# Reordering the opening of a one-core transformer block: four token tiles' first half, then the products of two weight groups

## The chip, the core and the metric

The kernel runs on one core of a Trainium2 chip. The core has five engines with a queue each: TensorE (PE in the profile; PEld is its weight load), VectorE (DVE), ScalarE (ACT), GpSimd (POOL) and SyncE (SP, which here only issues transfers). An engine takes its queue in order, and an instruction that waits for another engine holds up everything behind it. SBUF is the working memory; PSUM holds what TensorE writes (this kernel keeps eight tiles of 128 x 512 float32 there, one to a bank). The metric is the device time of one execution in microseconds (us).

## The reference

One encoder layer on x of 1024 tokens x 1024 features:

```
h = layer_norm(x, ln_in_g, ln_in_b)
proj = h @ w_in                      # 1024 x 11776
att  = dilated_attention(q, k, v of proj)
rec  = hgrn2(q, f_fwd, f_bwd, i, g of proj)
merged = sigmoid(ga) * (att @ w_att_up) + sigmoid(gh) * (rec @ w_hgrn_up)
h = layer_norm(ALPHA * h + merged @ w_o, ln1_g, ln1_b)
h = layer_norm(ALPHA * h + swiglu(h), ln2_g, ln2_b)
```

The change is in the first two lines and in where the normalised x is taken from for `ALPHA * h`.

## The kernel before

**Precision.** Every float32 operand of a matmul is split into a high part (`hi`, a cast on ScalarE, L205) and a low part (`lo`, a subtraction on GpSimd or VectorE, L209). A product of two split operands is three matmuls (`mm3`, L255 to L257): hi·hi, hi·lo, lo·hi.

**Blocks.** The product with `w_in` is done by a Strassen-Winograd scheme of seven products instead of eight, on 2 x 2 blocks. The activations are transposed (features on partitions). `b11` and `b21` are the two halves of the features for tokens 0 to 511 (token tiles 0 to 3, 128 tokens each), `b12` and `b22` those for tokens 512 to 1023 (tiles 4 to 7), and `t1` = b12 - b11, `t2` = b22 - t1, `t3` = b22 - b12, `t4` = b21 - t2 are their sums. The weights of a pair of column tiles are `a11`, `a12`, `a21`, `a22` (512 x 128 each, one DMA of 256 KB each in `block`), with the sums `s1` to `s4`. `PRODUCTS` pairs them: product 1 is a11·b11, 2 is a12·b21, 6 is s2·t2, 5 is s1·t1, 7 is s3·t3, 3 is s4·b22, 4 is a22·t4. Each product is 4 x 3 = 12 matmuls of 128 x 128 by 128 x 512.

**The stream of products.** `stream` is a generator. A weight group n is two pairs of column tiles (g = 0, 1); there are 23 groups. The order within a group is `ORDER` = 1, 2, 6, 5, 7, 3, 4, each product for g = 0 and then for g = 1. `prep(i)` writes the split of product i's weights three products ahead (four buffers each for `w_hi` and `w_lo`), `sums` the weight sums, `bank` picks the PSUM bank, `keep` copies a bank to SBUF, and the functions of `tiles` carry the results out (`evac`).

**The opening.** `phase0` loads the eight tiles of x, takes the statistics of each (`bn_stats` on VectorE, the power -0.5 on GpSimd), normalises it on ScalarE, stores the normalised tile to `ah_d` in DRAM, transposes it on TensorE by halves of 512 features (`transposed`, L285), scales the four 128 x 128 pieces of a half out of PSUM (`v`, partly on ScalarE, L293, partly on VectorE, L295: `on_act` says which), and splits the blocks. Tiles 4 to 7 also form t1 to t4. In the text of the program the eight tiles come one after the other, both halves each, with two products put in after four tiles.

**What sets the order.** The program is written once, and a list scheduler that models the engines puts each engine's instructions in order. Parts of the code written under `high_priority` go ahead; `add_manual_dep` (in `ordered` and `behind`) fixes that one instruction stands behind another. So the text does not tell the order, and below it is shown as the built program has it.

**Later.** `phase1` runs the stream and, between products, the recurrence and the attention as "side" work. Near its end `residual` reads the normalised x back, scales it and stores it to `ahs_d` for the second layer norm.

## Time and profile before

| | us |
|---|---|
| median of 3 runs | 2134.19 |
| the three runs | 2123.66 to 2137.27 |
| the profiled execution, time | 2131.49 |
| the profiled execution, span | 2129.7 |
| PE busy in the span | 2029.0 (95%) |
| DVE, POOL, ACT busy | 1392.7, 1077.5, 919.7 |

The span runs from the first to the last instruction of the profiled execution; its own time is 1.8 us longer. A busy PE is one that has a matmul under way, which says nothing of the clock it runs at: the granted clock stands apart. The views are read in stretches of the span, since the opening, where PE starts and stops, is a small part of it.

### The profile page before, as it was taken

The page shows a single profiled execution, that of the slowest core. Times are in us where ns is not written, and L with a number is a line of the kernel's source. Part 1 is how long each engine was busy: PE and PEld are TensorE (multiplying, and loading weights), DVE is VectorE, ACT ScalarE, POOL GpSimd, SP SyncE. Part 2 cuts the span into 40 slices and gives each one's busy share as a digit, 9 for nine tenths or more (in the row PEclk, how much of TensorE's full clock was granted, in tenths as well). Part 3 has the DMA queues.
Part 4 walks back from the last instruction along what each step waited for, and adds up shares of the span by engine and source line. Part 5 has one row for each costly group of instructions (what it writes and reads, how often), then busy time and mean ns, then how long its engine had stood idle before and what let it go on. Part 6 is the DMA issues. An engine that isn't in the chain of part 4 may idle for free.

```text
span 2129.7 us, 30900 instructions
## 1 busy us (share of the span) xinstructions
PE 2029.0 (95%) x10941; PEld 1674.6 (79%) x10941; DVE 1392.7 (65%) x2228; ACT 919.7 (43%) x1864; POOL 1077.5 (51%) x882
## 2 busy tenths in 40 slices
PE   4799999999999999999999899999999999999998
PEld 3678787788878788887888688878788888887876
DVE  7667746777459753788536712337867677767778
ACT  6544455434544435543355432135433333343542
POOL 3466653567536664465644754443656566630012
PEclk9899999999999999999999999999999999999999
DMA  5342442435424343333444755244434344348423
GB/s 202 109 133 95 147 155 73 144 118 167 130 92 141 135 146 125 124 129 109 146 130 142 283 188 164 89 139 139 154 109 153 129 144 134 117 160 291 158 89 124
DMA packets 273885, 301.10 MB, mean 141 GB/s; under 512 B 14081, under 2 KB 205378, under 8 KB 273730
## 3 DMA queue, kind: packets, MB, share of 16 engines
q1 hardware_dynamic: 266272, 273.73, 39.7%
q10 hardware_dynamic: 7458, 25.40, 3.0%
q8 instruction: 86, 1.41, 0.3%
q14 instruction: 69, 0.57, 0.1%
HBM read 200.25 MB, written 98.83 MB: 140 GB/s over the span
## 4 chain that ended last, share of the span: by engine, by line
PE 77%; DVE 12%; issue 5%; POOL 3%; DMA 2%; ACT 2%; SPq 0%; ACTq 0%; DVEq 0%; POOLq 0%
PE pj L255 17%; PE pj L256 17%; PE pj L257 16%; PE sd L256 6%; PE sd L255 6%; PE sd L257 6%; PE sd L1049 2%; POOL w_lo L209 1%; DVE qd L964 1%; DVE qd L967 1%; PE sd L998 1%; DVE p L849 1%; PE sd L863 1%; DVE fb L953 1%; ACT p L827 1%
## 5 line engine op out<-in xcount | busy, mean ns | idle before, releaser
L209 POOL TENSOR_TENSOR w_lo<-wa,w_hi 128x512 fp32r<-128x512 f32 x276 | 377.4, 1374 | 297.9 <-ACT w_hi L205 274.0
L205 ACT CAST w_hi<-wa 128x512 fp32r<-128x512 f32 x276 | 170.4, 619 | 245.8 <-PE pj L256 159.5
L209 POOL TENSOR_TENSOR w_lo<-wsum,w_hi 128x512 fp32r<-128x512 f32 x88 | 129.0, 1474 | 113.0 <-PE sd L257 60.4
L200 POOL TENSOR_TENSOR mv<-mv,mhalf 128x1 f32<-128x1 f32 x24 | 15.5, 647 | 228.6 <-DVE mv L199 225.5
L209 POOL TENSOR_TENSOR w_lo<-f_raw,w_hi 128x512 fp32r<-128x512 f32 x66 | 102.1, 1555 | 55.4 <-ACT w_hi L205 54.2
L255 PE MATMUL pj<-xt1hi,w_hi 128*128 128x512 f32 x260 | 103.9, 400 | 16.3 <-ACT xt1hi L205 10.7
L205 ACT CAST w_hi<-wsum 128x512 fp32r<-128x512 f32 x88 | 54.7, 621 | 124.6 <-PE sd L256 114.4
L255 PE MATMUL pj<-xb22hi,w_hi 128*128 128x512 f32 x260 | 102.6, 394 | 1.1 <-ACT wkeep L511 1.1
L256 PE MATMUL pj<-xt1lo,w_hi 128*128 128x512 f32 x260 | 102.3, 393 | 0.0
L257 PE MATMUL pj<-xt1hi,w_lo 128*128 128x512 f32 x260 | 102.0, 392 | 0.0
L256 PE MATMUL pj<-xb22lo,w_hi 128*128 128x512 f32 x260 | 101.5, 390 | 0.0
L257 PE MATMUL pj<-xb22hi,w_lo 128*128 128x512 f32 x260 | 101.3, 390 | 0.0
L209 POOL TENSOR_TENSOR w_lo<-ws,w_hi 128x512 fp32r<-128x512 f32 x46 | 63.0, 1373 | 69.2 <-ACT w_hi L205 63.3
L205 ACT CAST gwsum<-a_raw 128x512 fp32r<-128x512 f32 (+1 forms) x78 | 47.8, 616 | 102.9 <-PE pj L256 48.0
L511 ACT COPY wkeep<-pj 128x512 f32<-128x512 f32 x138 | 80.1, 582 | 22.1 <-DVE evh L430 10.1
L403 DVE TENSOR_TENSOR evh<-wkeep,pj 128x512 f32<-128x512 f32 x66 | 57.5, 879 | 48.5 <-PE pj L257 35.2
L209 DVE TENSOR_TENSOR gwkeep<-a_raw,gwsum 128x512 fp32r<-128x512 f32 (+1 forms) x78 | 57.7, 739 | 43.1 <-ACT gwsum L205 40.2
L489 POOL TENSOR_TENSOR wa<-wa,wa 128x512 f32<-128x512 f32 x46 | 67.6, 1480 | 35.6 <-DVE ws L488 27.6
L414 DVE TENSOR_TENSOR evh<-wkeep,pj 128x512 f32<-128x512 f32 x48 | 32.6, 681 | 80.7 <-PE pj L257 65.5
L255 PE MATMUL pj<-xt4hi,w_hi 128*128 128x512 f32 x192 | 77.8, 406 | 5.6 <-DVE evh L403 5.6
L257 PE MATMUL pj<-xt2hi,w_lo 128*128 128x512 f32 x192 | 76.1, 397 | 4.9 <-POOL w_lo L209 4.9
L255 PE MATMUL pj<-xb11hi,w_hi 128*128 128x512 f32 x192 | 77.3, 404 | 2.6 <-DVE evh L414 1.4
(406 smaller groups left out, 6587.1 us busy)
## 6 DMA issues: line engine op xcount, KB each, us to landing
wa<-in_w_in_dram SPq DMA_DIRECT2D x184, 256.0 KB, 3.1
f_raw<-in_w_ffn_in_dram SPq DMA_DIRECT2D x44, 512.0 KB, 4.2
a_raw<-gd SPq DMA_DIRECT2D x30, 512.0 KB, 3.5
gd<-fc SPq DMA_DIRECT2D x44, 256.0 KB, 2.0
gd<-fs SPq DMA_DIRECT2D x33, 256.0 KB, 2.1
tg<-evh SPq DMA_DIRECT2D x32, 256.0 KB, 3.5
tg<-tg SPq DMA_DIRECT2D x16, 512.0 KB, 3.7
y<-ahs SPq DMA_DIRECT2D x16, 512.0 KB, 5.5
```

What stands on the lines that cost most here:

```text
L205: nc.scalar.copy(hi, src)
L209: ins = e.tensor_sub(lo, src, hi.bitcast(F32))
L255: nc.tensor.matmul(ps, whi, xhi, start=first, stop=False, **kw)
L256: nc.tensor.matmul(ps, whi, xlo, start=False, stop=False, **kw)
L257: nc.tensor.matmul(ps, wlo, xhi, start=False, stop=last, **kw)
L403: self.left(nc.vector.tensor_tensor(o, self.order_src(add, g, kind), s, OP.add))
L414: self.left(nc.vector.tensor_add(t, add, ps))
L489: nc.gpsimd.tensor_sub(a["a21"], a["a11"], a["a21"])
L511: nc.scalar.copy(t, ps)
L827: nc.scalar.activation(z, z, AF.Exp, bias=N0[p, hd, tt:tt + 1], scale=QSCALE, accum_out=L0[p, hd, tt:tt + 1])
L849: nc.vector.tensor_scalar(z, z, W0[p, hd, tt:tt + 1], None, op0=OP.mult)
L1049: nc.tensor.matmul(po[:, jj, :], l, r, start=(n == 0), stop=(n == len(terms) - 1))
```

## The change

Six things, all in or for the opening:

1. `phase0` is written anew. It does the first half (b11) of tiles 0 to 3 first, then the products of b11, then their second half (b21), then tiles 4 to 7. The products are drawn from the stream inside it.
2. `stream` begins with product 1 of weight groups 0 and 1 and product 2 of groups 0 and 1, eight products in all, and then takes the other five of each group. Group 1's `a11` and `a12` are loaded for this into tiles of their own (`wfirst`) and loaded once more for its sums later. Some products go to the other PSUM banks (`sd`).
3. `transposed` gives a bank of four pieces to one engine (all four on ScalarE, or all four on VectorE), or takes two banks where both engines share a half (tile 3).
4. The three small steps behind the statistics go to GpSimd; the scale and shift are kept for all tiles (`mv0`).
5. The normalised tiles are no longer stored to `ah_d`. `residual` reads x again and normalises it once more on ScalarE.
6. `behind` and `ordered` fix some places: transposes of the second half behind the last product drawn, statistics of tiles 4 to 7 behind certain splits, the casts of the first weights behind certain casts of b11. The small parameters are loaded and transposed in two parts.

```diff
-    def transposed(self, pool, n, q, g, b, v=None, bufs=2, on_act=(1, 3, 6)):
+    def transposed(self, pool, n, q, g, b, v=None, bufs=2, on_act=(1, 3, 6), two=False, gate=None):
         ps = self.ps_sd()
+        pa = self.ps_sd() if two else ps
         for k in range(4):
-            nc.tensor.transpose(ps[:, 128 * k:128 * (k + 1)], n[:, 128 * (4 * q + k):128 * (4 * q + k + 1)],
-                                self.ident)
+            p = pa if 4 * q + k in on_act else ps
+            ins = nc.tensor.transpose(p[:, 128 * k:128 * (k + 1)], n[:, 128 * (4 * q + k):128 * (4 * q + k + 1)],
+                                      self.ident)
+            if gate:
+                self.behind(ins, gate)
...
+        def stats(tt):
+            st = self.tiny.tile([128, 2, 6], F32, name="bn0", tag="bnst", bufs=3)
+            for j in range(2):
+                ins = nc.vector.bn_stats(st[:, j, :], xs[tt][0][:, HALF * j:HALF * (j + 1)])
+                if tt > 3:
+                    self.behind(ins, at["lo", 3, "b11" if tt < 6 else "b21"])
+            mv = self.mv0[:, tt, :]
+            nc.vector.bn_aggr(mv[:, 0:2], st)
+            nc.gpsimd.tensor_scalar(mv[:, 2:3], mv[:, 1:2], LN_EPS, None, op0=OP.add)
+            nc.gpsimd.tensor_tensor(mv[:, 2:3], mv[:, 2:3], self.mhalf[:, 0:1], OP.pow)
+            nc.gpsimd.tensor_scalar(mv[:, 3:4], mv[:, 0:1], mv[:, 2:3], -1.0, op0=OP.mult, op1=OP.mult)
...
+        turn(3, 0, v[3][0], (2, 3))
+        put(3, "b11", v[3][0])
+        self.gates = [at["hi", 1, "b11"]] * 2 + [at["hi", 3, "b11"]] * 2
+        run(2)
+        for tt in range(4):
+            if tt < 3:
+                norm(tt + 1, 1)
+            turn(tt, 1, v[tt][1], DVE if tt % 2 else ACT, self.product)
+            self.left(put(tt, "b21", v[tt][1]))
             if tt == 1:
-                self.rest()
-            mv = self.stats(pool, xt, "0")
-            self.normalise(pool, xt, xt, mv)
-            nc.scalar.dma_start(self.ah_d[tt], xt)
...
+                load(2)
+                run()
+                stats(4)
+        self.rest()
+        run(3)
+        for tt in range(4, 8):
+            b11, b21 = v[tt - 4]
+            norm(tt, 0)
+            norm(tt, 1)
+            t1, t2 = xs[tt][1]
             _, (b12, b22) = hold("vt")
-            self.transposed(pool, xt, 0, gc, bc, b12, on_act=(0, 1, 3))
+            turn(tt, 0, b12, DVE if tt % 2 else ACT)
             nc.vector.tensor_sub(t1, b12, b11)
-            put("t1", t1)
-            self.transposed(pool, xt, 1, gc, bc, b22, on_act=(4, 5, 7))
+            if tt < 7:
+                stats(tt + 1)
+            turn(tt, 1, b22, ACT if tt % 2 else DVE)
             nc.vector.tensor_sub(t2, b22, t1)
-            put("t2", t2)
...
+            put(tt, "t2", t2)
+            nc.gpsimd.tensor_sub(b12, b22, b12)
+            nc.vector.tensor_sub(b21, b21, t2)
+            v[tt] = t1, b12, b22, b21
+            if tt > 4:
+                late(tt - 1, 0)
+            run()
+        late(7, 0)
+        for i in range(1, 4):
+            for tt in range(4, 8):
+                late(tt, i)
...
     def residual(self, pool, vecs):
...
-            nc.sync.dma_start(a, self.ah_d[tt])
+            nc.sync.dma_start(a, self.x[128 * tt:128 * (tt + 1), :])
+            mv = self.mv0[:, tt, :]
+            nc.scalar.activation(a, a, AF.Identity, bias=mv[:, 3:4], scale=mv[:, 2:3])
             nc.vector.scalar_tensor_tensor(a, a, ALPHA, gb, op0=OP.mult, op1=OP.mult)
...
-        seq = [(n, g, p) for n in range(len(tiles) // 4) for p in self.ORDER for g in range(2)]
+        O = self.ORDER
+        order = [(n, (p,)) for p in O[:2] for n in (0, 1)]
+        order += [(n, O[2:] if n < 2 else O) for n in range(len(tiles) // 4)]
+        seq = [(n, g, p) for n, part in order for p in part for g in range(2)]
...
+            if n == 1 and p == 2:
+                first[g, 2] = self.block(1, g, "a12", pool)
             with early(n):
                 ready[i] = self.granules()
-                self.split(*ready[i], A[g][self.PRODUCTS[p][0]])
+                self.split(*ready[i], first[g, p] if n == 1 and p < 3 else A[g][self.PRODUCTS[p][0]],
+                           key="w" if i < 4 else None)
...
-        def bank(n, g, b):
-            return self.ps_pj(2 * g + (n + b) % 2)
+        def bank(n, g, p):
+            if (n, p) in ((0, 5), (0, 2), (1, 2)):
+                return self.ps_sd()
+            return self.ps_pj(2 * g + (n + (p == 1)) % 2)
```

In `turn` the argument `act` lists the pieces that ScalarE takes (`ACT` is all four, `DVE` none), and `late` splits t1, t3, b22 and t4 of a tile. Line numbers of the changed program are some 11 to 120 higher: L255 to L257 are L268 to L270 there, L285 is L300, L205 is L212, L209 is L220, L295 is L312.

**The start of TensorE's queue**, before: transposes of x (`xt`) into PSUM (`sd`), and then the first product.

```order
L174 MATMUL sd<-tabs_sb,vrows 128x65
L285 MATMUL sd<-tabs_sb,xt 128x128 x40
L255 MATMUL pj<-xb11hi,w_hi 128x512 x2
L285 MATMUL sd<-tabs_sb,xt 128x128 x8
L256 MATMUL pj<-xb11lo,w_hi 128x512
L257 MATMUL pj<-xb11hi,w_lo 128x512
```

The same place in the changed program.

```order
L181 MATMUL sd<-tabs_sb,vrows_254 128x16
L300 MATMUL sd<-tabs_sb,xt 128x128 x16
L268 MATMUL pj<-xb11hi,w_hi 128x512 x3
L269 MATMUL pj<-xb11lo,w_hi 128x512
L270 MATMUL pj<-xb11hi,w_lo 128x512
```

Forty-eight of the 64 transposes stood ahead of the first whole product; now 16 do, and the other 48 stand between products.

**TensorE's queue where the first products of tokens 512 to 1023 come**, before: the end of product 2 of group 0 (the fourth product of the program), and what follows it.

```order
L256 MATMUL pj<-xb21lo,w_hi 128x512
L257 MATMUL pj<-xb21hi,w_lo 128x512
L255 MATMUL pj<-xt1hi,w_hi 128x512 x2
L255 MATMUL pj<-xt2hi,w_hi 128x512 x2
L256 MATMUL pj<-xt1lo,w_hi 128x512
```

In the changed program: the end of product 2 of group 1 (the eighth product), the last eight transposes, and product 6 of group 0.

```order
L269 MATMUL sd<-xb21lo,w_hi 128x512
L270 MATMUL sd<-xb21hi,w_lo 128x512
L300 MATMUL sd<-tabs_sb,xt 128x128 x8
L268 MATMUL pj<-xt2hi,w_hi 128x512 x2
L269 MATMUL pj<-xt2lo,w_hi 128x512
```

Four products of group 1, 48 matmuls, moved ahead of this point, and t2 is now the first block wanted of the second half of the tokens.

**VectorE's queue at that place in the changed program**: the work on tile 7 (`v_287` is its partner b11, `v_288` its b21; `vt` are the scaled pieces) up to the low part of its t2, and what stands behind.

```order
L312 TENSOR_SCALAR vt<-sd,vc 128x128 x4
L422 TENSOR_TENSOR xt<-vt,v_287 128x512
L426 TENSOR_TENSOR xt<-vt,xt 128x512
L429 TENSOR_TENSOR v_288<-v_288,xt 128x512
L220 TENSOR_TENSOR xt2lo<-xt,xt2hi 128x4x128
L220 TENSOR_TENSOR xt1lo<-xt,xt1hi 128x4x128 x2
L220 TENSOR_TENSOR xt3lo<-vt,xt3hi 128x4x128 x4
L220 TENSOR_TENSOR xb22lo<-vt,xb22hi 128x4x128 x4
L220 TENSOR_TENSOR xt4lo<-v_282,xt4hi 128x4x128
```

The low parts of t3, b22 and t4, which stood among those of t1 and t2 before, now stand behind the last t2.

**ScalarE's queue in `residual`**, before: casts of weights (`w_hi`), copies and evacuations (`wkeep`, `evh`), with the stores of `a`.

```order
L205 CAST w_hi<-wa_10853 128x512
L511 COPY wkeep<-pj 128x512
L205 CAST w_hi<-ws_11295 128x512
L374 DMA ahs_115<-a_11464 128x1024
L415 ACTIVATE evh<-evh 128x512
```

And in the changed program.

```order
L212 CAST w_hi<-wa_10851 128x512
L633 COPY wkeep<-pj 128x512
L452 ACTIVATE a_11462<-a_11462,mv_203 128x1024
L212 CAST w_hi<-ws_11293 128x512
L496 ACTIVATE evh<-evh 128x512
L452 ACTIVATE a_11535<-a_11535,mv_203 128x1024
```

A normalisation that waits for the load of its `a` now stands ahead of a cast of weights; there are eight such places. Apart from the opening and this stretch, the engines' orders are nearly the same in both programs.

251 lines of the change are left out of this document (148 added, 103 removed).

## The prediction

> **What bounds the kernel now.** I read the page's slices first, then the first 140 us in stretches of 10 and 20, then TensorE's waits there, then its single matmuls.
>
> ```profile
> PE   4799999999999999999999899999999999999998
> ```
>
> PE is busy nine tenths or more in nearly every fortieth (53 us) of the span; the first two hold the largest gap, and the change works there. The stretches, with each engine's busy time and number of instructions:
>
> ```profile
> core 0: us, PE busy (x) PEld busy (x) DVE busy (x) ACT busy (x) POOL busy (x), PEclk, DMA share, GB/s
> 30.00:40.00 10.00, 4.57 (x14) 2.65 (x14) 10.00 (x19) 7.03 (x17) 3.32 (x2) 1.00 0.09 38
> 40.00:50.00 10.00, 9.79 (x39) 8.15 (x40) 9.64 (x20) 8.31 (x18) 4.03 (x2) 1.00 0.05 17
> 50.00:60.00 10.00, 5.52 (x29) 4.32 (x27) 10.00 (x16) 9.70 (x23) 4.35 (x3) 0.95 0.16 63
> 60.00:70.00 10.00, 1.99 (x4) 1.00 (x4) 10.00 (x18) 5.42 (x10) 0.19 (x3) 0.50 0.26 79
> 70.00:80.00 10.00, 10.00 (x40) 7.89 (x39) 3.35 (x6) 3.81 (x7) 2.97 (x4) 0.87 0.11 31
> 100.00:120.00 20.00, 18.12 (x84) 14.73 (x83) 19.71 (x16) 8.88 (x16) 17.45 (x17) 1.00 0.26 93
> 120.00:140.00 20.00, 18.85 (x91) 15.68 (x90) 12.07 (x14) 10.28 (x19) 11.35 (x9) 1.00 0.61 187
> ```
>
> From 30 to 70 us VectorE never rests (39.6 of 40) and TensorE mostly does. At 70 VectorE has done its share and PE is full. So VectorE bounds the opening. TensorE's own waits up to 140 us say the same (total, times, longest): the longest product wait is for the last token tiles' t1, and after the opening it loses little.
>
> ```profile
> PE pj L255 <- ACT xt1hi L205: 10.7, 1, 10.7
> ...
> PE pj L257 <- POOL w_lo L209: 1.9, 1, 1.9
> ```
>
> The matmuls themselves (start, duration):
>
> ```profile
> 40.98 0.78 PE L256 MATMUL pj<-xb11lo,w_hi 128*128 128x512 f32 x1
> ...
> 45.39 0.40 PE L257 MATMUL pj<-xb11hi,w_lo 128*128 128x512 f32 x1
> ...
> 48.12 1.03 PE L285 MATMUL sd<-tabs_sb,xt 128*128 128x128 f32 x8
> ...
> 55.13 0.39 PE L257 MATMUL pj<-xb21hi,w_lo 128*128 128x512 f32 x1
> ```
>
> ```profile
> 66.23 1.22 PE L255 MATMUL pj<-xt1hi,w_hi 128*128 128x512 f32 x2 [10.71 <-ACT xt1hi L205]
> 69.24 1.22 PE L255 MATMUL pj<-xt2hi,w_hi 128*128 128x512 f32 x2 [1.79 <-ACT xt2hi L205]
> 70.39 0.80 PE L256 MATMUL pj<-xt1lo,w_hi 128*128 128x512 f32 x1
> 70.98 0.63 PE L257 MATMUL pj<-xt1hi,w_lo 128*128 128x512 f32 x1
> 71.41 0.63 PE L255 MATMUL pj<-xt1hi,w_hi 128*128 128x512 f32 x1
> ...
> 72.69 0.40 PE L255 MATMUL pj<-xt1hi,w_hi 128*128 128x512 f32 x1
> ...
> 76.78 0.39 PE L257 MATMUL pj<-xt2hi,w_lo 128*128 128x512 f32 x1
> ```
>
> The rows from 72.69 to 76.78 are 18 steps: 0.227 us a matmul. Before 72.69, and before 45.39, a step is 0.43 (70.98 to 71.41): half the rate. The first four products (48 matmuls: products 1 and 2 of group 0, for both pairs) end at 55.1; then PE rests 10.7 us, and runs without a gap from 72.7, when 48 + 2 + 2 + 5 = 57 matmuls are done. I measure an opening by its **lag**, the time at which PE runs unbroken less the time that its finished matmuls need at full rate: 72.7 - 57 x 0.227 = **59.7 us**. The total of matmuls doesn't change, so the change is worth the difference in lag plus what it alters later.
>
> **The change, part by part.** *First products.* The 16 transposes and the products of b11 wait for the fourth b11 cast on ScalarE.
>
> ```profile
> 9.35 1.24 ACT L278 ACTIVATE xt<-xt,mv 128x1024 f32<-128x1024 f32 x1 [2.49 <-DVE mv L277]
> ...
> 50.64 1.51 ACT L293 ACTIVATE vt<-sd,vc 128x128 f32<-128x128 f32 x4
> ```
>
> ```profile
> L205 ACT CAST w_hi<-wa 128x512 fp32r<-128x512 f32 x276 | 170.4, 619 | 245.8 <-PE pj L256 159.5
> ```
>
> Up to that cast ScalarE has seven half normalisations (0.62, half of 1.24), six pieces (0.38) and six casts (0.62): 10.3 us, from about 9.35, gives 19.7 us; before, the first low-part matmul ran at 41.0. The eight stores of the normalised tiles leave ScalarE's queue. TensorE then needs 48 x 0.227 = 10.9, 2 more at half rate, and 16 transposes between (8 take 1.03): 35 us. The first product of b21 waits for the last low part of b21, behind four `bn_stats` on VectorE, some 3 us more; 48 matmuls and 24 transposes take 14. The eighth product ends near 35 + 3 + 14 = 52 us.
>
> *t2, which decides.* What VectorE must do from 19.7 us until the low part of the last t2, by its changed queue: 34 subtractions and additions, 24 pieces, 8 `bn_stats`, 4 aggregations.
>
> ```profile
> 12.15 0.21 DVE L198 BATCH_NORM_AGGREGATE mv<-bn 128x2 f32<-128x12 f32 x1
> ...
> 36.24 1.27 DVE L191 BATCH_NORM_STATS2 bn<-xt 128x6 f32<-128x512 f32 x2
> ...
> 50.39 1.43 POOL L209 TENSOR_TENSOR w_lo<-wa,w_hi 128x512 fp32r<-128x512 f32 x1 [0.88 <-ACT w_hi L205]
> ...
> 50.58 1.78 DVE L355 TENSOR_TENSOR vt<-vt 128x512 f32<-128x512 f32 x1
> ...
> 57.29 1.63 POOL L209 TENSOR_TENSOR w_lo<-ws,w_hi 128x512 fp32r<-128x512 f32 x1 [2.17 <-ACT w_hi L205]
> ...
> 57.72 0.67 DVE L428 TENSOR_TENSOR wkeep<-wkeep,pj 128x512 f32<-128x512 f32 x1
> ...
> 58.31 1.15 DVE L209 TENSOR_TENSOR xt3lo<-vt,xt3hi 128x512 fp32r<-128x512 f32 x1
> ...
> 59.39 0.72 DVE L295 TENSOR_SCALAR vt<-sd,vc 128x128 f32<-128x128 f32 x2
> ```
>
> ```profile
> 66.05 0.68 DVE L209 TENSOR_TENSOR xb22lo<-vt,xb22hi 128x512 fp32r<-128x512 f32 x1
> ...
> 66.65 0.68 DVE L361 TENSOR_TENSOR v<-v,vt 128x512 f32<-128x512 f32 x1
> ```
>
> 34 x 0.60 (66.05 to 66.65) + 24 x 0.36 + 8 x 0.64 + 4 x 0.2 = 20.4 + 8.6 + 5.1 + 0.8 = 34.9, so 54.6 us if it never waits. It waits, though: the b21 pieces of tiles 1 and 3 need transposes that stand behind the first and second product (about 2.5 us each), the first b21 low part waits for ScalarE (1.3), ScalarE's casts for weight buffers of a running product (1 to 2): 7 us. And GpSimd gets in its way. In the rows above a VectorE subtraction that begins within a GpSimd one ends 0.54 us after it (50.58 + 1.78 = 52.36, GpSimd ended at 51.82; 59.46 and 58.92), while an operation that reads PSUM isn't held (57.72, 0.67). The stretch has 16 such GpSimd operations. Each costs between nothing and 1.1 us (1.78 - 0.68), so 0 to 18; half of them meeting a subtraction at 0.5 (1.15 - 0.68) is 4, and I take that, since a third or so of VectorE's time here is pieces, evacuations and waits. Sum: 54.6 + 7 + 4 = **65.6 us** for the first whole product of t2, with 96 matmuls done. The bounds are 55 (no wait, no collision) and 80 (all of both).
>
> *Clock.* Between 52 and 65 PE rests again, so it starts at half rate as at 40.98 (4.4 us of it until 45.39) and at 70.39 (2.3 us). With 3.4 us, 8 matmuls, the lag is 65.6 + 3.4 - 104 x 0.227 = **45.4 us**; gain 59.7 - 45.4 = **14.3 us**. The Trainium skill ("TensorE: Matmul & The Clock Gate", Part 1) says that an idle window of about 3.4 us halves the clock and that about 3.4 us of steady work restores it; that speaks against a queue with more rests in it. By that rule each slow start loses 1.7 us, where the rows lose 2.2 (4.4 us at half rate) and 1.2 (2.3); and the rest of 3 us ahead of the b21 products would only just escape a slow start of its own, with which the gain would be 12.6 us and not 14.3. The trace agrees that a long rest halves the clock (0.50 in 60 to 70 us), and no row here shows one of 3 us.
>
> *After t2.* VectorE still has 14 low parts (8.4 us); PE has 11 us of products 6 and 5 meanwhile, so these are hidden. They cost up to 8 if it had not. Product 6 of group 1 now follows group 0 at once, where products 1 and 2 gave its weight sums time, and half of it stands on GpSimd behind a step of the recurrence. Before, the same hand-over lost 20 - 18.12 + 20 - 18.85 = 3.0 us of PE in 100 to 140 us. I take the same, bounds 0 and 8.
>
> *residual.* Eight normalisations of 1.24 us come to ScalarE, each waiting in its queue for a load of x.
>
> ```profile
> 1200.00:1210.00 10.00, 7.54 (x32) 5.86 (x33) 8.81 (x8) 4.88 (x9) 8.66 (x6) 1.00 0.92 330
> 1210.00:1220.00 10.00, 7.13 (x33) 5.58 (x31) 9.93 (x8) 5.23 (x9) 7.39 (x5) 0.98 0.44 160
> ```
>
> ```profile
> DMA to landing us min/median/max: 3.8/5.7/9.1
> ```
>
> The second row is the load of `a` before (L371). ScalarE is half idle there, but casts of weights and evacuations stand behind the wait, and PE already loses 2.5 and 2.9 us in these two stretches. Bounds: nothing, if the loads have landed; 8 x (9.1 - 5.7) = 27 if each came as late as the latest. Nearest to nothing, since only three or four loads are issued shortly before: I take 2. The eight stores that go, the banks given to one engine (they remove some of the 39.6 us of VectorE's work order, not of its work) and the three small GpSimd steps lie beside VectorE's chain and count as nothing; without that cover the small steps would add to each tile's start.
>
> **Sum.** 2131.5 (the profiled execution) - 14.3 + 0 + 2 = **2119 us**. That execution is 2.7 us below the median of the runs shown, 2134.2, whose spread is 13.6; so 0.6% faster by the one, 0.7% by the other. About 1% is what a measurement of this kernel can tell from no change.
>
> **Rivals.** *VectorE's chain is shorter*: its waits overlap the collisions and t2 starts at 58. The lag is 58 + 3.4 - 23.6 = 37.8, the gain 22, the time 2110. For it: 7 and 4 us are put one after the other; against it: VectorE rests nowhere from 30 to 70 us now. Chance 0.2.
>
> *The change doesn't do what it says*: VectorE has about the same work before t2 is whole and every GpSimd operation collides; t2 starts at 80, the lag is 80 + 3.4 - 23.6 = 59.8, and the eight early products only fill time that was lost anyway: 2131.5 + 2, about 2133. For it: GpSimd has 16 operations there against seven before in 30 to 60 (2, 2 and 3 in the stretches). Chance 0.12.
>
> *Slower*: in `residual`, ScalarE waits in line for x, the casts of weights behind it come late, and TensorE stops for each. With the 27 us above, 2131.5 - 14.3 + 27 = 2144; with half the opening's gain gone as well, 2151, over 1% slower above 2153 to 2155. It decides from 14 us of added waits on. For it: TensorE's two thin stretches above, with the transfers at 330 GB/s and 0.92 of their time; against it, ScalarE's 4.88 of 10. Chance 0.08.
>
> **How the numbers follow.** The forecast has 0.60, with a range of its own of 2112 to 2127. The whole range, 2107 to 2136, takes in the short chain and the lost gain and leaves out most of the slow case. Faster by over 1% is the short chain and a little of the forecast's lower end, 0.22. Slower by over 1% is the upper part of the slow case and what I don't see, 0.07. Within 1%: 0.71.
>
> **What would show it.** PE's first matmul of b11 near 20 us and eight products done by 51 to 53; a second rest of PE until about 65, ended by xt2hi or xt2lo; unbroken matmuls from about 69; VectorE busy without a rest from 38 to 73. In `residual`, stretches of PE no thinner than 7 of 10. I am wrong if PE stops within the eight products for PSUM (`sd` is shared by transposes and products), if t2 starts before 58 or after 75, or if PE's busy time from 1160 to 1240 falls by more than 5 us.

## The result, and the profile after

The changed kernel takes **2118.1 us** (median of 6 executions, 2109.2 to 2120.4). The kernel before, timed beside it, takes 2131.9 us (6 executions, 2123.7 to 2137.3). The ratio is 0.9938, with an interval of 0.9919 to 0.9957, so the change makes the kernel about 0.6% faster. A second timing gave 2118.8 us (6 executions, 2114.7 to 2121.6) and a ratio of 0.9952 (0.9936 to 0.9967). The profiled execution took 2119.32 us with a span of 2117.4 us, which is 12.3 us less than before (2129.7). The prediction was 2119 us.

The total is as predicted. Its parts aren't. The slices of the changed kernel's page (TensorE's busy tenths in 40 slices) show where the time came from: the first slice is fuller (6 tenths, 4 before), the second has 7 as before, and elsewhere little moves.

```profile
PE   6799999999999999999999999999999999999998
```

The stretches of the changed kernel, with the columns that the stretches of before have (start and end; busy time and number of instructions of PE, PEld, DVE, ACT and POOL; PE's granted clock; DMA share; GB/s):

```profile
30.00:40.00 10.00, 7.89 (x43) 6.25 (x42) 7.00 (x12) 9.58 (x23) 4.51 (x4) 1.00 0.31 99
40.00:50.00 10.00, 8.64 (x41) 6.90 (x40) 10.00 (x21) 3.70 (x7) 8.74 (x10) 1.00 0.00 1
50.00:60.00 10.00, 5.71 (x29) 4.10 (x27) 9.96 (x12) 6.78 (x13) 6.63 (x5) 0.84 0.21 79
60.00:70.00 10.00, 0.00 (x0) 0.00 (x0) 9.42 (x17) 4.78 (x12) 3.12 (x2) 0.50 0.25 79
70.00:80.00 10.00, 9.56 (x34) 7.37 (x35) 10.00 (x16) 9.27 (x18) 2.59 (x2) 0.81 0.00 0
100.00:120.00 20.00, 19.13 (x88) 15.50 (x87) 20.00 (x14) 9.98 (x18) 19.51 (x16) 1.00 0.57 171
120.00:140.00 20.00, 20.00 (x90) 16.58 (x89) 16.07 (x16) 7.75 (x15) 15.01 (x12) 1.00 0.53 173
```

From 40 to 80 us VectorE is still the busy engine (39.4 of 40 us), and TensorE still has its long rest, now all of 60 to 70. GpSimd has become much busier in 40 to 60 (15.4 us; 8.4 before). In 100 to 140 TensorE loses 0.87 us, where it lost 3.03 before.

TensorE's waits up to 140 us (total, times, longest) and then its matmuls at the places that the prediction names:

```profile
PE pj L268 <- ACT xt2hi L212: 10.6, 1, 10.6
...
PE sd L269 <- DVE xb21lo L220: 1.4, 1, 1.4
PE sd L268 <- ACT xb21hi L212: 1.2, 1, 1.2
...
PE pj L270 <- POOL w_lo L220: 0.9, 1, 0.9
PE pj L269 <- DVE xt2lo L220: 0.4, 1, 0.4
```

```profile
19.84 1.65 PE L268 MATMUL pj<-xb11hi,w_hi 128*128 128x512 f32 x3 [2.30 <-ACT xb11hi L212]
...
37.12 0.50 PE L268 MATMUL sd<-xb21hi,w_hi 128*128 128x512 f32 x1 [1.19 <-ACT xb21hi L212]
...
41.66 0.50 PE L269 MATMUL sd<-xb21lo,w_hi 128*128 128x512 f32 x1 [1.36 <-DVE xb21lo L220]
...
53.58 0.39 PE L270 MATMUL sd<-xb21hi,w_lo 128*128 128x512 f32 x1
...
70.03 1.22 PE L268 MATMUL pj<-xt2hi,w_hi 128*128 128x512 f32 x2 [10.65 <-ACT xt2hi L212]
71.66 0.79 PE L269 MATMUL pj<-xt2lo,w_hi 128*128 128x512 f32 x1 [0.41 <-DVE xt2lo L220]
...
73.90 0.40 PE L268 MATMUL pj<-xt2hi,w_hi 128*128 128x512 f32 x1
```

The first b11 product starts at 19.84. The eighth product ends at 53.97. Then TensorE rests until t2 comes: its high part at 70.0, its low part at 71.7. From 73.90 it runs at the full rate, with 96 + 7 = 103 matmuls done. Its lag is 73.9 - 103 x 0.227 = **50.5 us**, where before it was 59.7. The opening therefore gives **9.2 us**, and not 14.3.

The other terms can be read from the **lead**: how much earlier the changed kernel's profile has the same number of products' matmuls (128x512) done. It is 11.2 us at 160 to 230 us (9.2 from the opening, about 2 from the hand-over in 100 to 140), 8.7 at 300, 8.2 at 1140, 11.1 at 1200, 9.75 at 1560 to 1860 and 12.0 at the end.

### The profile page after: what moved, and what is told of

Its sections match the earlier page's. It is cut to its first block, busy times and chain, and to the rows that moved or that the text cites. A ratio compares the mean times of both kernels' runs of the same rounds, so it can differ in the third digit from the quotient of the medians.

```text
span 2117.4 us, 30907 instructions
## 1 busy us (share of the span) xinstructions
PE 2027.0 (96%) x10942; PEld 1673.0 (79%) x10942; DVE 1396.8 (66%) x2214; ACT 925.9 (44%) x1870; POOL 1100.3 (52%) x903
## 3 DMA queue, kind: packets, MB, share of 16 engines
q8 instruction: 86, 1.41, 0.3%
## 4 chain that ended last, share of the span: by engine, by line
PE 56%; DVE 6%; DMA 2%; issue 2%; ACT 1%; POOL 1%; SPq 0%; ACTq 0%; DVEq 0%; POOLq 0%
PE pj L269 11%; PE pj L268 11%; PE pj L270 11%; PE sd L269 6%; PE sd L268 6%; PE sd L270 6%; PE sd L1158 1%; DMA a<-in_x_dram 1%; ACT p L936 1%; DVE qd L1073 1%; DVE qd L1076 0%; PE sd L1107 0%; POOL w_lo L220 0%; DVE p L958 0%; DVE fb L1062 0%
## 5 line engine op out<-in xcount | busy, mean ns | idle before, releaser
L220 POOL TENSOR_TENSOR w_lo<-wa,w_hi 128x512 fp32r<-128x512 f32 x272 | 375.3, 1387 | 286.1 <-ACT w_hi L212 256.3
L212 ACT CAST w_hi<-wa 128x512 fp32r<-128x512 f32 x272 | 167.9, 619 | 249.2 <-PE pj L269 130.8
L220 POOL TENSOR_TENSOR w_lo<-wsum,w_hi 128x512 fp32r<-128x512 f32 x88 | 128.7, 1471 | 113.5 <-PE sd L270 60.7
L220 POOL TENSOR_TENSOR w_lo<-f_raw,w_hi 128x512 fp32r<-128x512 f32 x66 | 102.0, 1554 | 55.7 <-ACT w_hi L212 54.5
L208 POOL TENSOR_TENSOR mv<-mv,mhalf 128x1 f32<-128x1 f32 x16 | 10.7, 677 | 207.3 <-DVE mv L207 207.2
L212 ACT CAST w_hi<-wsum 128x512 fp32r<-128x512 f32 x88 | 54.7, 622 | 124.8 <-PE sd L269 114.6
L268 PE MATMUL pj<-xt1hi,w_hi 128*128 128x512 f32 x252 | 101.3, 402 | 4.5 <-DVE evh L484 3.7
L268 PE MATMUL pj<-xb22hi,w_hi 128*128 128x512 f32 x252 | 99.5, 395 | 0.0
L270 PE MATMUL pj<-xt1hi,w_lo 128*128 128x512 f32 x252 | 99.3, 395 | 0.0
L270 PE MATMUL pj<-xb22hi,w_lo 128*128 128x512 f32 x252 | 98.4, 391 | 0.3 <-POOL w_lo L220 0.3
L220 POOL TENSOR_TENSOR w_lo<-ws,w_hi 128x512 fp32r<-128x512 f32 x46 | 64.7, 1411 | 64.8 <-ACT w_hi L212 60.1
L212 ACT CAST gwsum<-a_raw 128x512 fp32r<-128x512 f32 (+1 forms) x78 | 47.7, 616 | 100.6 <-PE pj L269 43.5
L268 PE MATMUL pj<-xt2hi,w_hi 128*128 128x512 f32 x192 | 78.0, 407 | 13.1 <-ACT xt2hi L212 10.6
L220 DVE TENSOR_TENSOR gwkeep<-a_raw,gwsum 128x512 fp32r<-128x512 f32 (+1 forms) x78 | 57.8, 741 | 41.0 <-ACT gwsum L212 38.1
L268 PE MATMUL pj<-xt4hi,w_hi 128*128 128x512 f32 x192 | 77.8, 405 | 5.8 <-DVE evh L484 5.8
L268 PE MATMUL pj<-xb11hi,w_hi 128*128 128x512 f32 x192 | 77.3, 404 | 3.4 <-ACT xb11hi L212 2.3
L495 DVE TENSOR_TENSOR evh<-wkeep,pj 128x512 f32<-128x512 f32 x45 | 30.7, 683 | 71.7 <-PE pj L270 49.0
```

What stands on the lines that cost most here:

```text
L212: ins = nc.scalar.copy(hi, src) if eng_hi == "act" else nc.vector.tensor_copy(hi, src)
L220: ins = e.tensor_sub(lo, src, hi.bitcast(F32))
L268: nc.tensor.matmul(ps, whi, xhi, start=first, stop=False, **kw)
L270: self.product = nc.tensor.matmul(ps, wlo, xhi, start=False, stop=last, **kw).ins.name
L495: self.left(nc.vector.tensor_add(t, add, ps))
```

## The experiments

Where a median is given, the number of executions stands behind it, and ratios are to the kernel before on the same chip. The other experiments are one profiled execution each and are read by their rows only. "t2 after b11" is the time from the first b11 product to the low part that makes t2 whole; it is used since the first b11 product alone moves by 1 us or so from run to run. In the changed kernel it is 71.6 - 19.8 = 51.8 us; in its repeat, 51.5.

**1. Only the order of the products undone.** The opening keeps its new order of tiles, engines and queues. The products go back to "group 0 whole, then group 1", and group 1's early loads of weights go with them.

```diff
-        order = [(n, (p,)) for p in O[:2] for n in (0, 1)]
-        order += [(n, O[2:] if n < 2 else O) for n in range(len(tiles) // 4)]
+        order = [(n, O) for n in range(len(tiles) // 4)]
...
-        run(3)
+        run(2)
```

> The changed kernel with one part undone: the products of each weight group stand in the order of before (group 0 whole, then group 1), so four products and not eight run ahead of t2. Theory (VectorE's chain to the last low part of t2 sets the end of the opening, and the early products fill time that TensorE would lose): the chain loses the evacuations of two products, some 3 us, so t2 is whole at 68 to 69 us and not at 71.7, but only 48 matmuls are done by then, so the lag is 57 to 59 us against 50.5 in the changed kernel: 7 to 8 us slower than it, about 2126. The hand-over at 100 to 140 us loses again what it lost before (3 us): 2128. Rival (the early products themselves hold up t2, by TensorE's queue and the PSUM banks that their sums and the transposes share): t2 is whole near 60 us and the lag about the same as in the changed kernel, the time 2118.

Median 2127.6 us (10), ratio 0.9998 (0.9982 to 1.0013). t2 even comes sooner, at 66.7 us (48.3 after b11), but only four products are done by then. TensorE reaches its full rate at 69.48 with 56 matmuls done, so the lag is 69.5 - 56 x 0.227 = 56.8 us and the gain 2.9. At 120 to 220 us its lead is 2.6. The hand-over loses 3.1 us again, as this stretch of it shows (columns as above):

```profile
100.00:120.00 20.00, 16.91 (x82) 13.80 (x82) 20.00 (x17) 6.39 (x11) 18.10 (x17) 1.00 0.08 30
```

The early products of group 1 carry the gain: by the medians, the rest of the rearranged opening, alone, is worth nothing that can be measured. The profiled execution says less than the medians here. At 2121.8 us it is the fastest of the ten, and it ends 10 us ahead of the profile of before. The order of products also sets the hand-over, which I had priced as untouched.

**2. The stores of the normalised tiles back, and `residual` reads them.** ScalarE then has eight stores in the opening and no normalisation in `residual`.

```diff
+            if q:
+                nc.scalar.dma_start(self.ah_d[tt], xs[tt][0])
...
-            nc.sync.dma_start(a, self.x[128 * tt:128 * (tt + 1), :])
-            mv = self.mv0[:, tt, :]
-            nc.scalar.activation(a, a, AF.Identity, bias=mv[:, 3:4], scale=mv[:, 2:3])
+            nc.sync.dma_start(a, self.ah_d[tt])
```

> The changed kernel with the eight stores of the normalised tiles back in the opening, and the second reading from these instead of from x, without the eight normalisations on ScalarE. Theory (the change of what is read is worth the 3 us by which the changed kernel's lead grew between 1180 and 1200 us, from 8.2 to 11.1): the lead stays at about 8 us there, the whole is 2 to 3 us slower, 2121; in the opening the stores lie on ScalarE's queue in the shadow of other work, t2 whole at 71 to 73 us. Rival (that gain comes from where this stretch now falls against the weight stream, not from what is read): the lead still grows by 2 to 3 us and the time is 2118. As my prediction priced it, the normalisations cost 2 us, and without them the kernel would be 2 us faster, 2116.

Median 2122.4 us (10), ratio 0.9978 (0.9961 to 0.9994). t2 after b11 is 51.8 us, the same as without the stores, so their removal is worth nothing, as priced. In `residual` the sign is the other way round: the lead falls from 9.4 us at 1140 to 6.85 at 1200, where the changed kernel's rises from 8.2 to 11.1. The second normalisation, priced at a loss of 2 us, is a gain.

**3. Is it what is read, or the pass on ScalarE?** As experiment 2, but ScalarE passes over each loaded tile once, with scale 1 and bias 0 (some padding beside the constants goes, to make room for these two).

```diff
             nc.sync.dma_start(a, self.ah_d[tt])
+            nc.scalar.activation(a, a, AF.Identity, bias=self.same[:, 4:5], scale=self.same[:, 0:1])
```

> The normalised tiles are stored in the opening and read back, as in the kernel before, but the second reading has a pass of ScalarE over each tile all the same (times one, plus nothing) ahead of VectorE's two steps. It tells whether the 3 us that the changed kernel gains near 1190 us come from what is read or from the pass on ScalarE. Theory (the pass paces the stretch: it holds VectorE's long steps apart, so that the weight casts and GpSimd's low parts come in time): TensorE waits 4 to 5 us between 1140 and 1240 us, as in the changed kernel (4.3), and the lead grows by 2 to 3 us there. Rival (the reading of x itself is better, by its transfers): TensorE waits 7 to 8 us there, as before (7.1) and with the stored tiles (8.0).

The lead rises from 8.3 us to 11.1, as in the changed kernel. It is the pass itself that helps. TensorE's waits from 1130 to 1240 us (total, times, longest), in the changed kernel, in experiment 2 and in this one, those ahead of products alone:

```profile
PE pj L268 <- ACT wkeep L633: 2.4, 1, 2.4
...
PE pj L270 <- POOL w_lo L220: 1.9, 2, 1.0
```

```profile
PE pj L271 <- POOL w_lo L221: 4.5, 2, 2.9
PE pj L269 <- ACT wkeep L634: 3.5, 2, 2.8
```

```profile
PE pj L272 <- ACT wkeep L638: 2.4, 1, 2.4
PE pj L274 <- POOL w_lo L224: 2.4, 2, 1.5
PE pj L272 <- DVE evh L500: 0.3, 1, 0.3
```

These are 4.3, 8.0 and 5.1 us; before it was 7.1 (4.6 for `w_lo`, 1.4 for `evh`, 1.1 for `wkeep`), and in the repeat of the changed kernel 5.1. A look at ScalarE's queue shows how that can be, first in experiment 2 and then in this one:

```profile
1173.62 1.05 ACT L213 CAST att_hi<-st_raw 128x1024 fp32r<-128x1024 f32 x1 [5.85 <-DMA tg<-evh]
...
1174.58 0.61 ACT L213 CAST w_hi<-wa 128x512 fp32r<-128x512 f32 x1
```

```profile
1170.45 0.62 ACT L216 CAST w_hi<-wa 128x512 fp32r<-128x512 f32 x1 [2.65 <-PE pj L273]
...
1171.46 1.05 ACT L216 CAST att_hi<-st_raw 128x1024 fp32r<-128x1024 f32 x1
```

Without the pass, a cast of another stage that waits 5.85 us for a transfer stands ahead of a cast of weights. With the pass, the two stand the other way round and the weights come 4.1 us sooner. That the order of these two casts is the cause is read from the rows; it was not changed alone. The sign does not hang on one execution: from 1140 to 1240 us the lead rises by 1.2 to 4.4 us in all 12 profiles with a pass (2.5 in the changed kernel, 1.2 in its repeat), and it falls by 2.7 in experiment 2 alone.

**4. GpSimd's step beside the chain moved to VectorE.** For each tile, t3 = b22 - b12 stands on GpSimd, and VectorE's next steps, t2 = b22 - t1 (line 426) and t4 = b21 - t2 (line 429), can run beside it.

```diff
-            nc.gpsimd.tensor_sub(b12, b22, b12)
+            nc.vector.tensor_sub(b12, b22, b12)
```

> The changed kernel with the four subtractions for t3 on VectorE, where they stand right ahead of the first subtraction for t4, and not on GpSimd beside it. Theory (the two engines get in each other's way: the t4 step takes 1.65 us only because GpSimd's t3 step starts at the same moment): the t4 step falls to 0.7 us in all four tiles, the t3 step adds 0.6 us each, and t2 is whole 1 to 2 us earlier, near 70 us. Rival (VectorE's time there is its own instructions and their number counts): the t4 step stays near 1.6 us, and t2 is whole 2.4 us later, near 74 us.

VectorE's and GpSimd's rows of the changed kernel for tiles 6 and 7, each behind one row of tile 4, show what was to be tested (start, duration):

```profile
49.91 1.70 DVE L429 TENSOR_TENSOR v<-v,xt 128x512 f32<-128x512 f32 x1
...
62.01 0.69 DVE L422 TENSOR_TENSOR xt<-vt,v 128x512 f32<-128x512 f32 x1 [0.17 <-ACT vt L310]
62.73 0.69 DVE L426 TENSOR_TENSOR xt<-vt,xt 128x512 f32<-128x512 f32 x1
63.46 1.64 DVE L429 TENSOR_TENSOR v<-v,xt 128x512 f32<-128x512 f32 x1
...
69.36 1.64 DVE L429 TENSOR_TENSOR v<-v,xt 128x512 f32<-128x512 f32 x1
```

```profile
49.79 1.28 POOL L220 TENSOR_TENSOR w_lo<-wa,w_hi 128x512 fp32r<-128x512 f32 x1
...
62.78 1.77 POOL L428 TENSOR_TENSOR vt<-vt 128x512 f32<-128x512 f32 x1 [4.09 <-DVE xt L422]
...
68.65 1.81 POOL L428 TENSOR_TENSOR vt<-vt 128x512 f32<-128x512 f32 x1 [4.10 <-DVE xt L422]
```

The subtraction of line 429 takes 1.64 us and ends at 65.10, which is 0.55 us after GpSimd's line 428 (64.55), and again at 71.00 after 70.46. VectorE's low part of t2 stands behind it and starts at 65.02 and 70.93. Line 428 doesn't wait for t2: what releases it is line 422 (t1), the last to read the buffer that t3 overwrites. So it starts right beside line 426, which began first and isn't held, and line 429 then begins inside it. In tiles 4 and 5 line 429 is held too (1.70 and 1.65 us), but by a low part of weights. In the experiment the rows of line 429 for tiles 6 and 7 are these:

```profile
62.02 0.69 DVE L429 TENSOR_TENSOR v<-v,xt 128x512 f32<-128x512 f32 x1
...
67.45 0.69 DVE L429 TENSOR_TENSOR v<-v,xt 128x512 f32<-128x512 f32 x1
```

t2 comes 50.0 us after b11, 1.8 sooner, though VectorE has four subtractions more. The collision is shown for tiles 6 and 7. In tiles 4 and 5 the same step stays at 1.41 and 1.77 us, beside low parts of weights on GpSimd, so the theory's "in all four tiles" doesn't hold.

**5. The last two tiles' t3 and t4 out of the way.** For tiles 6 and 7 both go to VectorE, behind the last low part of t2.

```diff
-            nc.gpsimd.tensor_sub(b12, b22, b12)
-            nc.vector.tensor_sub(b21, b21, t2)
+            if tt < 6:
+                nc.gpsimd.tensor_sub(b12, b22, b12)
+                nc.vector.tensor_sub(b21, b21, t2)
...
+                if tt > 5 and i in (1, 3):
+                    _, b12, b22, b21 = v[tt]
+                    ins = nc.vector.tensor_sub(b12, b22, b12) if i == 1 else nc.vector.tensor_sub(b21, b21, xs[tt][1][1])
+                    self.behind(ins, at["lo", 7, "t2"])
```

> The changed kernel with the t3 and t4 steps of the last two token tiles taken off VectorE's and GpSimd's way to t2: both on VectorE, behind the last low part of t2. Theory (VectorE's queue sets t2): the two t4 steps (1.6 us each) go and two waits of 0.6 us for the cast on ScalarE show, so t2 is whole near 69.7 us, 1.9 us earlier, the lag 48.6; the four steps take 2.6 us behind t2 and are hidden by the two products of t2 (5.5 us); whole time 2 us less than the changed kernel. Rival (tiles 6 and 7 wait for their buffers or for ScalarE): t2 stays at 71 to 72 us. Rival (what is put off comes due at once): TensorE stops by 2 us or more between the products of t2 and t3, and nothing is gained.

t2 comes 49.4 us after b11, 2.3 sooner than in the changed kernel. But at 115.33 us TensorE waits 2.6 us for a low part of weights from GpSimd and then runs matmuls at half rate, so the stretch from 100 to 120 has 17.23 us of PE at a clock of 0.91, and the lead at 120 is 11.8 us, no more than without the edit.

**6. Everything that t2 doesn't need behind it.** All t3, the t4 of tiles 6 and 7 and the sums of weights for the next products stand behind VectorE's last low part.

```diff
-            put(tt, "t2", t2)
-            nc.gpsimd.tensor_sub(b12, b22, b12)
-            nc.vector.tensor_sub(b21, b21, t2)
+            self.left(put(tt, "t2", t2))
+            if tt < 6:
+                nc.vector.tensor_sub(b21, b21, t2)
...
+                _, b12, b22, b21 = v[tt]
+                if i == 1:
+                    self.behind(nc.vector.tensor_sub(b12, b22, b12), at["lo", 7, "t1"])
+                elif i == 3 and tt > 5:
+                    self.behind(nc.vector.tensor_sub(b21, b21, xs[tt][1][1]), at["lo", 7, "t1"])
```

> The changed kernel with everything put behind the last low part of t2 that t2 doesn't need: all four t3 steps (on VectorE then), the t4 steps of tiles 6 and 7, and the two sums for product 3 (s4). Theory (VectorE's queue and the held subtractions set t2): besides the 1.6 us that the t4 steps of tiles 6 and 7 gave, the s4 sums bring 1.7 us and GpSimd without t3 some 1 to 2 us, so t2 is whole 4 to 5 us earlier than in the changed kernel, counted from the first b11 product (47 us instead of 51.8). Behind t2 stand 8 more steps (4.8 us) ahead of the low parts of t3, which are due 11 us after t2: hidden. Lead over before 15 to 17 us at 100 to 150 us. Rival (what is put off comes due at once): TensorE waits 2 us or more for t1 or t3 low parts, and the lead is 13.

t2 comes 47.0 us after b11, 4.8 sooner, and the lead at 100 us is 14.5. At 120 it is 12.0. What takes it back is this matmul of the experiment, and the GpSimd rows ahead of it:

```profile
115.19 0.50 PE L270 MATMUL pj<-xt3hi,w_lo 128*128 128x512 f32 x1 [2.99 <-POOL w_lo L220]
```

```profile
110.53 2.95 POOL L1062 TENSOR_SCALAR t<-t,gna,ga 128x1024 f32<-128x1024 f32 x1 [0.60 <-ACT fb L1061]
113.45 1.69 POOL L220 TENSOR_TENSOR w_lo<-wa,w_hi 128x512 fp32r<-128x512 f32 x1
```

A step of the recurrence stands on GpSimd ahead of the low part, which ends at 115.1. In the changed kernel the low part behind the same step is this one:

```profile
114.89 1.29 POOL L220 TENSOR_TENSOR w_lo<-wa,w_hi 128x512 fp32r<-128x512 f32 x1
```

It ends at 116.2, and TensorE comes for it at 116.4, just in time. A t2 that is some us earlier is therefore paid back here.

**7. Three pieces of each half on ScalarE.** The pieces of tiles 4 to 7 are divided between the engines as before the change, which takes eight pieces, 8 x 0.325 = 2.6 us, from VectorE.

```diff
-            turn(tt, 0, b12, DVE if tt % 2 else ACT)
+            turn(tt, 0, b12, (0, 1, 3))
...
-            turn(tt, 1, b22, ACT if tt % 2 else DVE)
+            turn(tt, 1, b22, (0, 1, 3))
```

> The changed kernel with the pieces of tiles 4 to 7 divided as before: of each half three pieces on ScalarE and one on VectorE, out of the same PSUM bank, where the changed kernel gives a whole bank to one engine (four pieces of a tile to each). VectorE has two pieces less in each of four tiles. Theory (VectorE's queue sets t2): 8 pieces of 0.33 us go from VectorE, so t2 is whole up to 2.6 us earlier. Rival (one engine to a bank matters, since two engines at one bank hold each other up): the pieces take longer each, and t2 comes no earlier, or later by 1 to 3 us. My prediction priced this part at nothing.

t2 comes 51.3 us after b11, 0.4 less, about what two executions of the changed kernel differ by (0.3). VectorE now waits for ScalarE's pieces instead, as these rows of tile 7 show:

```profile
65.21 0.41 DVE L312 TENSOR_SCALAR vt<-sd,vc 128x128 f32<-128x128 f32 x1 [0.94 <-ACT vt L310]
65.91 0.41 DVE L312 TENSOR_SCALAR vt<-sd,vc 128x128 f32<-128x128 f32 x1 [0.29 <-ACT vt L310]
```

**8. Two of the small steps back from GpSimd to VectorE.**

```diff
-            nc.gpsimd.tensor_scalar(mv[:, 2:3], mv[:, 1:2], LN_EPS, None, op0=OP.add)
+            nc.vector.tensor_scalar(mv[:, 2:3], mv[:, 1:2], LN_EPS, None, op0=OP.add)
...
-            nc.gpsimd.tensor_scalar(mv[:, 3:4], mv[:, 0:1], mv[:, 2:3], -1.0, op0=OP.mult, op1=OP.mult)
+            nc.vector.tensor_scalar(mv[:, 3:4], mv[:, 0:1], mv[:, 2:3], -1.0, op0=OP.mult, op1=OP.mult)
```

> The changed kernel with two of the three small steps behind each tile's statistics (the one that adds the constant and the one that forms the shift) on VectorE again; only the power stays on GpSimd. My prediction counted the move to GpSimd as nothing. If so, the first product of b11 begins within 0.5 us of the changed kernel's, counted from the first normalisation, and t2 is whole within 1 us of 51.8 us after it. Rival (each such step costs GpSimd 0.5 to 1.2 us, VectorE only 0.1 to 0.2, and each tile's start waits for it): the first product of b11 comes 1 to 2 us earlier and t2 with it.

The first normalisation starts at 9.2 us (6.9 and 7.1 in the two profiles of the changed kernel), because the shift now stands in VectorE's queue behind the next tile's `bn_stats`, which end at 9.1. The first b11 product comes at 21.1 (19.8), but t2 is whole at 71.2 us, where it is whole at 71.6 and 71.3 in the changed kernel. So the move as a whole is worth nothing that shows at t2. Counted from the first normalisation, as the expectation does, the first product comes 0.8 to 1.1 us sooner and t2 2.2 to 2.7 us sooner, which is the rival's side. The edit moved the start as well and so doesn't separate the two: that the steps cost nothing on GpSimd is not shown.

**9. TensorE kept busy in its rest before t2.** Matmuls of b11 by itself, whose result nobody reads, fill the rest: 36 of them in one kernel, 30 in another.

```diff
+            if tt == 7:
+                ps, hi = self.ps_sd(), self.xb["b11"][0]
+                for _ in range(36):
+                    ins = nc.tensor.matmul(ps, hi[:, 0, 0:128], hi[:, 0, :], start=True, stop=True,
+                                           skip_group_check=True)
+                    self.behind(ins, self.turned_last)
```

> The changed kernel with 36 matmuls of b11 on itself put on TensorE behind the last transposes, where it rests before t2; nobody reads what they write. Theory (the granted clock falls in the rest, and the first matmuls of t2 pay for it): with the rest filled to within 2 us of t2, the products of t2 run at 0.227 us a matmul from the first one, t2 starts at the same time, and the lag falls by 1.5 to 2 us, from 50.5 to 49. Rival (the rate at the start is that of the waits for low parts, not of the clock): the first eight matmuls take 0.43 us each again and nothing changes. If the 36 run beyond t2's start, it is late by what is left of them.

> The changed kernel with 30 idle matmuls in TensorE's rest before t2 (36 ended 1.1 us behind t2's last low part), nothing else changed. It tells whether the single time of 2111.7 us of the run with 36 was the filled rest or chance. Theory (the fill is worth the half-rate start alone, 7 to 13 matmuls of 0.2 us, and that run's further 5 us at 400 us came from a rest that was shorter by chance): median 1 to 3 us below the changed kernel, ratio to before 0.993 to 0.995, and a lead of 13 to 14 us at 120 to 150. Rival (the fill keeps TensorE faster later on too): ratio 0.991 or less.

With 36, t2's products run at full rate from the first one, as these rows show, and the lead at 120 us is 13.4:

```profile
60.85 11.03 PE L430 MATMUL sd<-xb11hi 128*128 128x512 f32 x36 [2.52 <-DVE vt L313]
71.72 0.61 PE L268 MATMUL pj<-xt2hi,w_hi 128*128 128x512 f32 x2
```

That execution took 2111.7 us. The gain isn't borne out: with 30, which end as t2's high part comes and leave no half rate there either, the median is 2121.2 us (7, 2112.3 to 2123.0; ratio 0.9962, 0.9948 to 0.9977), no better than the changed kernel. In its profile the opening does gain: the lag is 47.4 us and the lead at 100 us 14.4. Then TensorE waits for the same low part as in experiment 6, and the lead is 12.6 at 120:

```profile
114.76 0.80 PE L270 MATMUL pj<-xt3hi,w_lo 128*128 128x512 f32 x1 [3.18 <-POOL w_lo L220]
```

The slow start at t2 is real (7 to 13 matmuls at half rate, in every run without a fill), but to take it away isn't worth anything that these timings show.

**10. All of it together, and the changed kernel again.** Experiment 6, with 20 idle matmuls, and GpSimd's second long step of the recurrence placed behind the low part that TensorE waited for. Beside it the changed kernel, unedited.

```diff
-        nc.gpsimd.tensor_scalar(t3, t3, gna, ga, op0=OP.mult, op1=OP.add)
+        ins = nc.gpsimd.tensor_scalar(t3, t3, gna, ga, op0=OP.mult, op1=OP.add)
+        if h == 0 and d == 1:
+            self.behind(ins, self.wlo[1, 1, 7])
```

> Three edits on the changed kernel together: what t2 doesn't need stands behind its last low part (as in the run that put off t3, t4 and s4), 20 idle matmuls of b11 on itself fill TensorE's rest before t2, and on GpSimd the second long step of the first recurrence stands behind the low parts of group 1's product 7, for which TensorE waited 3.0 us at 112 us when t2 came earlier. Theory (opening bound by VectorE's queue, then the clock at its start, then GpSimd's queue at the hand-over): the lead over before, 12.9 us at 120 to 150 us in the changed kernel, becomes 4.5 (t2) and 1.5 (clock) more, 17 to 19 us, if the hand-over gives nothing back; the time is 4 to 6 us below the changed kernel's, ratio 0.991 to before. Rival (the recurrence is what bounds the hand-over, and its step put off is late itself): TensorE waits there as long for something else, and the lead at 150 us is 12 to 13 as in the three runs before; ratio 0.994.

> The changed kernel once more, beside the run with the three edits, so that the two are compared on the same chip: ratio to before 0.992 to 0.996, as before. Its profile also shows how much of the lead after 150 us is chance: if the rests of 2 to 3.6 us (at about 395, 712, 959, 1206 us) cost TensorE's clock at other places than in the first profile, the lead at 480 and at 1900 us differs by some us from 9.2 and 12.0, while it is the same within 1 us at 150.

The combination takes 2115.7 us (6, 2111.5 to 2119.5), ratio 0.9936 (0.9918 to 0.9953); the changed kernel beside it 2118.8 us, 0.9952 (0.9936 to 0.9967). Its lead is 14.7 us at 100 and 14.6 at 120, but 11.5 at 160, where the changed kernel has 11.2 and its repeat 9.9. TensorE's waits for low parts of weights up to 140 us are now four that sum to 4.0 us. So the rival of the expectation came true: with the step put off, TensorE waits as long at other places. The other runs point the same way. In the twelve profiles with the early products the lag goes from 45.0 to 52.4 us, but the lead at 160 us only from 9.1 to 12.2, and the four shortest lags (45.0 to 48.9) have leads of 9.3 to 11.5. The combination is faster than the kernel before. That it is faster than the changed kernel is not shown, as the intervals overlap.

## Why the prediction was right, point by point

**The sum was right by luck: its errors cancel.** The opening gave 9.2 us, and 14.3 was predicted. The hand-over gave about 2 where no change was predicted, and `residual` gave 2.9 where a loss of 2 was predicted. That is 5.1 us too much in the one term and 2.2 + 4.9 = 7.1 too little in the others. The rest of the difference, 2 us, goes between the stages: in the first profile the lead falls by 2.5 us from 230 to 300 us and moves again after 1200, and in the repeat it is 12.8 at 420 to 600 and 9.8 at the end. Since two profiles of the same kernel differ there, I put this down to single executions and not to the change.

**Held: what bounds the opening.** VectorE works almost without a rest from 40 to 70 us (29.4 of 30), and TensorE waits for it. Experiments 4, 5 and 6 each take work or collisions from that chain, and t2 comes 1.8, 2.3 and 4.8 us sooner. The rival with a shorter chain (t2 at 58) falls: t2 was whole at 71.6.

**Held: the mechanism of the gain.** Eight products instead of four are done before the rest. With four, the gain is gone (experiment 1, ratio 0.9998). The rival that the early products "only fill time that was lost anyway" falls: the lag fell by 9.2 us.

**Held: the first products and the work of VectorE.** The first b11 product starts at 19.84 us (19.7 predicted), the eighth ends at 53.97 (52). From 19.8 to 71.6 us VectorE's chain has 35 subtractions of 0.60 (34 predicted), 24 pieces of 0.325, eight `bn_stats` of 0.60 and four aggregations of 0.12: 34.1 us (34.9 predicted). It is idle for 7.6 us (7 predicted).

**Failed: "half of them meeting a subtraction at 0.5 is 4".** Eleven subtractions were held, and the time that they took over 0.68 us sums to 8.6 us, twice the term: eleven and not eight, at 0.78 us each and not 0.5. Each of them begins inside a GpSimd operation and ends 0.55 us after it. Six meet a low part of weights (5.3 us), four meet line 428 (3.2), one a sum of weights (0.1). The error was to count collisions as chance meetings. In tiles 6 and 7 line 428 is released by VectorE's own line 422, and lines 426 and 429 stand right behind that, so line 429 is held each time. In tiles 4 and 5 GpSimd comes to line 428 later, and it holds a sum of weights and line 426. Another 1.5 us are small gaps and steps a little longer than these means, which the sum had at nothing. So 34.1 + 7.6 + 8.6 + 1.5 = 51.8 us from the first b11 product to t2, where 45.9 was predicted, and t2 was whole at 71.6 us and not 65.6. The stretch stayed within the bounds that I gave it (55 and 80). The Trainium skill ("SBUF — State Buffer", section "SBUF: two separate sides") describes an exclusive lock on a port that the two engines share, for VectorE operations with two SBUF inputs and GpSimd operations that read SBUF: the later one waits for the whole of the earlier. The trace agrees that the later one is held: in tiles 6 and 7 line 429 begins 0.7 us after GpSimd's line 428 and ends 0.55 us after it, and line 426, which began first, takes its 0.69 us.

**Failed in size: the slow start.** I took 3.4 us for 8 matmuls. The changed kernel had 7 slow ones, full rate 2.2 us after t2 was whole. The repeat had 13. This is of the order predicted, and varies.

**Failed: "I take the same, bounds 0 and 8" for the hand-over.** TensorE lost 0.87 us there and not 3.0, and with the order of products undone it lost 3.1 again (experiment 1). I had named the new neighbours in the queue but not asked when TensorE would come for each low part. The place is on a knife's edge: in the changed kernel the low part is done 0.2 us before TensorE comes, and with t2 sooner by 2.3 or 4.8 us TensorE waits 2.6 to 3.0 us for it. What in turn holds GpSimd up there is open: with the step of the recurrence put off, the waits moved and summed to 4.0 us (experiment 10). This also says why 5 us more in the opening, which experiment 6 reached, are not 5 us at the end.

**Failed in sign: `residual`, "I take 2".** The eight normalisations were priced as a wait that stands ahead of casts. They do stand there, but by their place they also change which cast comes next on ScalarE. The two stretches that I quoted went from 7.54 and 7.13 us of TensorE to this in the changed kernel:

```profile
1200.00:1210.00 10.00, 6.86 (x23) 5.21 (x24) 7.83 (x5) 3.79 (x6) 9.13 (x6) 0.85 0.49 169
1210.00:1220.00 10.00, 10.00 (x45) 8.22 (x44) 3.04 (x4) 4.90 (x9) 6.97 (x5) 0.98 0.55 195
```

Since the changed kernel is 8 us ahead there, the same stretches don't hold quite the same work. Over the 80 us from 1160 to 1240 TensorE is busy for 72.96 us before, 75.65 in the changed kernel, 74.87 in its repeat and 72.01 in experiment 2. The slower rival, which lived on this term, falls: the pass makes the stage shorter (experiments 2 and 3), and the store-and-read version is the one that loses.

**Held: two items priced at nothing.** These are the stores (experiment 2, t2 after b11 unchanged at 51.8) and the division of the pieces (experiment 7, 0.4 us). Of the third, the small steps on GpSimd, only the sum with what the edit moved beside them is nothing (experiment 8).

**The signs.** The eight products were done at 53.97 us (51 to 53 named), TensorE ran at full rate from 73.9 (69), and one stretch of `residual` was at 6.86 (7 or more). One sign of being wrong came up in small: between the products TensorE stopped 0.9 us for a PSUM bank (the transposes at 39.65 us, released by ScalarE's line 310). It then waited 1.4 us more for the low part of b21, so the bank didn't set the pace.

**The rule on the clock.** The Trainium skill ("TensorE: Matmul & The Clock Gate", Part 1) speaks of an idle window of about 3.4 us, and I read it as letting the products of b21 "only just escape" a slow start. In the changed kernel's profile they do (clock 1.00 from 30 to 50 us). In the repeat, 8 of their matmuls ran at half rate, though no rest among them was longer than 1.4 us; over the 12 runs with the early products it happened in 8. So the escape was luck, and the measurement decides: shorter rests can be enough. The price that I gave for it, 1.7 us, was wrong as well: TensorE rests anyway before t2, and the eighth product then ends some 0.5 to 1.8 us later after b11, ahead of the long rest.

## What to carry to other kernels

An engine that runs dry gains from work brought forward from a later stage, and the gain is read from what is finished when it starts again, not from when it starts again: experiment 1 had t2 5 us sooner and gained nothing. Where a VectorE step releases a GpSimd operation and VectorE's next subtractions follow at once, they meet each time (tiles 6 and 7); such meetings are to be counted one by one at their measured excess, not at a chance. Where an added operation waits in a queue, look at what it changes places with: in `residual` the order of two casts was worth more than the operation cost, and at the hand-over a t2 that came 2 to 5 us sooner cost a wait of 2.6 to 3.0 us.
